# Strassen block products for half of the value, key and query projections of a hybrid decoder step

## The chip, the cores and the metric

The kernel runs on one core of a Trainium2 chip. The core has a matrix engine (TensorE, PE in the profile, with its weight loads as PEld), a vector engine (VectorE, DVE), a scalar engine (ScalarE, ACT), a general one (GpSimd, POOL), and a queue that issues transfers (SyncE, SP). On-chip data lies in SBUF, matrix results in PSUM, which has eight banks of 512 float32 columns for each of 128 partitions. The metric is the device time of one execution in microseconds (us), the median of several runs.

## The reference

One inference step of a two-layer trunk, all in float32, for a prompt of 512 tokens and 8 sample sequences of 8 tokens, 576 tokens in all (`NT`). Layer 0 is a gated short convolution, layer 1 a matrix-memory block (mLSTM). The layer that the change touches:

```python
xm, z = jnp.split(h @ w_in, 2, axis=-1)          # 1024 -> 2048 each
xc, new_buf = causal_dwconv(xm, conv_buf, conv_w)
xc = jax.nn.silu(xc + conv_b)
q = xc @ w_q                                     # 2048 -> 2048
k = xc @ w_k                                     # 2048 -> 2048
v = xm @ w_v                                     # 2048 -> 2048
gates = jnp.concatenate([q, k, v], axis=-1) @ w_if + b_if
```

After it come the chunked recurrence over four heads with a 512 x 512 state per head and sequence, a norm per head, the gate `silu(z)` and the output projection. All outputs, the new states too, are returned.

## The kernel before

Tokens lie along the free dimension (576 columns), features along the 128 partitions, so a feature vector of 2048 is 16 tiles. A weight chunk is 8 blocks of 128 x 128 (1024 inputs by 128 outputs) and arrives in one transfer of 512 KB. The values have chunks 96 to 127, two for each of 16 output tiles; keys and queries alternate in chunks 128 to 191 (tile f: key 128 + 4f and 129 + 4f, query 130 + 4f and 131 + 4f).

Every float32 product is made of three faster ones: each operand is split into a rounded high part and the low rest (`split` for activations, `split_weights` for half a chunk: a cast on ScalarE, L167, and a subtraction on VectorE, L168), and `step` issues high x high, high x low and low x high, each for 256 and 320 columns, which lie in two banks of one accumulator (L182). So a chunk is 8 k steps of 6 matmuls. The raw weights have two buffers, the split halves three each.

The stages, in program order: layer 0 (chunks 0 to 79), the input projection of layer 1 ("xm", chunks 80 to 95, with the convolution on VectorE and a store of each convolved tile to the scratch `xcs`), the values, then keys and queries head by head in the order 3, 0, 1, 2, then the z tiles, the recurrence, the state update and the output projection. The `xm` tiles stay on chip as high and low parts (32 slots of a pool of `N_SLOT` equal ones), the convolved tiles too.

Small jobs ride along: `work` is a queue from which `run` takes one job at given k steps (`pops`, two a chunk in these stages). They are the transposes of a finished tile (`by_token`), the gate products, a head's scores, and eight state products per head (`query_state`), each of which loads two halves of a state tile of 512 KB each into the pool `C` of six buffers (L135). When the key of the last tile (head 2, tile 3) is done, the first eight tiles of the residual stream come back and are normalised (`second_norm`), four ahead of the last query tile's first chunk and four ahead of its second.

The order on each engine is written by a planner when the program is built: it keeps a clock of its own, and at each time gives an engine the earliest instruction of the program that its model calls ready; a tile gets its buffer in that order too. Each engine then runs its list in order and waits at semaphores. `issue_after` pins an instruction behind another one. All loads and stores go through the one queue of SP.

Of the kernel before, what the change touches and what calls it, by code (L numbers as in the profile page):

```python
# [48 lines left out]
N_SLOT = 69  # L49
# [5 lines left out]
CBUF = 6  # L55
# [10 lines left out]
def trunk(tc, io):  # L66
    nc = tc.nc
    ctx = ExitStack()
    with ctx:
# [4 lines left out]
        cpool = ctx.enter_context(tc.tile_pool(name="cpool", bufs=CBUF))  # L74
        psum = ctx.enter_context(tc.tile_pool(name="psum", bufs=2, space=PSUM))
# [12 lines left out]
        def mm(name="mm"):  # L88
            uid[0] += 1
            return psum.tile([P, 1024], F32, name=f"{name}{uid[0]}", tag="mm", bufs=2)  # L90
# [26 lines left out]
        last_hi = []  # L117
# [38 lines left out]
        def weight_tile():  # L156
            uid[0] += 1
            return wpool.tile([P, 8, P], F32, name=f"wr{uid[0]}", tag="raw", bufs=2)

        def split_weights(raw, i, keep=False):  # L160
# [6 lines left out]
            nc.scalar.copy(hi, raw[:, 4 * i:4 * i + 4, :])  # L167
# [31 lines left out]
        def gemm(chunk0, nchunk, xs, pops=()):  # L199
            acc = mm("acc")  # L200
            for c_ in range(nchunk):
                products(acc, weights(chunk0 + c_), xs[8 * c_:8 * c_ + 8], c_ == 0, c_ == nchunk - 1, pops)
            return acc

# [43 lines left out]
        def conv(cv, u, ext, taps):  # L248
# [3 lines left out]
            nc.vector.tensor_scalar(cv, u, taps[h], None, ALU.mult)  # L252
# [21 lines left out]

        warm_up(WARM)
# [104 lines left out]
        xm, xc = [], []  # L380
# [10 lines left out]
        for f in range(NW):  # L391
# [11 lines left out]
            xm.append(split(u))  # L403
            cv = T(name="xc")
            conv(cv, u, ext_f, [col(f"cb{j}", f) for j in range(4)])
            nc.gpsimd.tensor_copy(cpb[:, f, :], u[:, NP - 3:NP])
            nc.scalar.activation(cv, cv, AF.Silu, bias=col("cbias", f))
            store(out=xcs[f], in_=cv)
            xc.append(cv)
            if f % 4 == 3:  # L410
                store(out=io["exb_out"][f // 4], in_=ext)
        store(out=io["cpb_out"], in_=cpb)
# [43 lines left out]
        xcr = xc  # L456
        xc = []
        for h in range(NH):
            vt = []
            for dt in range(4):  # L460
                f = 4 * h + dt
                acc = gemm(96 + 2 * f, 2, xm, (3, 6))
                v = T(name="v")
                nc.scalar.copy(v, flat(acc))
                vt.append(v)
                dup = S([P, 256], name="dup")
                spread(v, dup)
                s = slice(128 * dt, 128 * dt + 128)
                work.append(lambda v=v, dup=dup, h=h, s=s: by_token(v, dup, 1.0, vps[h][:, :, s], vss[h][:, :, s]))
                if f >= 8:  # L470
                    xc.append(split(xcr[f - 8]))
            work.append(lambda h=h, vt=vt: gates(h, vt))
        xc.extend(split(t) for t in xcr[8:])

        Sc, qcs = {}, {}
        nst = const.tile([P, NH, 2, 4, 4], F32, name="nst")
# [18 lines left out]
        def unit(h, u, dt):  # L495
            uid[0] += 1
            halves = []
            for i in range(2):
                t = cpool.tile([P, 2, 512], F32, name=f"c{uid[0]}_{i}", tag="C")
# [35 lines left out]
        def sample_scores(st, u):  # L535
# [5 lines left out]
            if u == 1:  # L541
# [4 lines left out]
                Sc[st["h"]] = ss  # L546
# [8 lines left out]
        heads = [dict(h=h, kt=[], qt=[], kd=[], qp=[]) for h in range(NH)]  # L555
        for h in (3, 0, 1, 2):
            st = heads[h]
            for dt in range(4):
                f = 4 * h + dt
                acc = gemm(128 + 4 * f, 2, xc, (3, 6))  # L560
                k = T(name="k")
                nc.scalar.copy(k, flat(acc))  # L562
# [8 lines left out]
                if (h, dt) == (2, 3):  # L571
                    xs = []
                    for m in range(KD):
                        x = T(name="x")
                        load(out=x, in_=x1s[m])
                        xs.append(x)
                    second_norm(range(4))
                    run(len(work))
                    acc = mm("acc")
                    products(acc, weights(128 + 4 * f + 2), xc[0:8], True, False)  # L580
# [750 lines left out]
```

## Time and profile before

| | |
|---|---|
| median of 3 runs | 1751.58 us (1749.59 to 1751.87) |
| the profiled execution, its span | 1754.37 us, 1752.6 us |
| TensorE matmuls busy, count | 1728.1 us (99%), 12771 |
| VectorE, ScalarE busy | 824.1 us (47%), 574.7 us (33%) |
| mean granted TensorE clock | 0.989 |
| moved by the transfers | 268.95 MB, mean 153 GB/s |

The span runs from the first to the last instruction; the execution's own time has a little around it. Busy shares are averages over stages with different limits. A row of a group gives line, engine, operation, the names written and read, shapes and count, then busy time and the mean of one in ns, then the idle time ahead of these instructions and what ended it. A row in order of time starts with its start and length in us. A matmul's length contains the pipeline's depth, so the distance of starts, not the length, tells its cost in a stream.

### The profile page before, as it was taken

To read this page: it belongs to the slowest core of one execution; us is meant where nothing else is said; L and a number is where in the kernel's file an instruction comes from. 1 tells how busy PE (TensorE), PEld (TensorE's weight loads), DVE (VectorE), ACT (ScalarE), POOL (GpSimd) and SP (SyncE) were. 2 spreads that over 40 slices of the span, in tenths; PEclk is the share of its full clock that TensorE was granted. 3 is DMA by queue.
4 is the path that set the end of the run, shared out by engine and by line. 5 is a ranking of instruction groups with operands and counts; after the bars stand their busy time and mean duration, and the time that the engine had idled before them with its cause. 6 is when DMAs were issued, how large, how long until landed. Compare 5 with 4: busy or idle time off the path is not lost.

```text
span 1752.6 us, 30800 instructions
## 1 busy us (share of the span) xinstructions
PE 1728.1 (99%) x12771; PEld 1654.7 (94%) x12771; DVE 824.1 (47%) x1445; ACT 574.7 (33%) x1001; POOL 125.7 (7%) x273
## 2 busy tenths in 40 slices
PE   9999999999999999999999999999999998998998
PEld 9999999999999999999999899899899887998998
DVE  5645444454346962222423222222227666678765
ACT  5222222222233332232322222222225545545421
POOL 0000000000001100000000000000001112212200
PEclk9999999999999999999999999999999899999999
DMA  5222222223343443433333543633637377997983
GB/s 165 81 86 84 89 89 85 91 79 105 125 132 104 150 139 103 120 101 108 106 88 99 192 148 94 219 125 119 211 111 247 119 227 242 370 337 265 372 304 108
DMA packets 104317, 268.95 MB, mean 153 GB/s; under 512 B 10704, under 2 KB 33104, under 8 KB 104176
## 3 DMA queue, kind: packets, MB, share of 16 engines
q1 hardware_dynamic: 104176, 266.98, 46.8%
q8 instruction: 100, 1.64, 0.4%
q14 instruction: 41, 0.34, 0.1%
HBM read 205.63 MB, written 61.30 MB: 152 GB/s over the span
## 4 chain that ended last, share of the span: by engine, by line
PE 90%; DMA 5%; DVE 3%; ACT 1%; issue 1%; SPq 0%; POOL 0%; DVEq 0%
PE acc L182 79%; DMA cs_out<-c 2%; PE qa L510 2%; DVE c L868 1%; PE r L867 1%; DMA cp_out<-cp 1%; DMA c<-cs 1%; PE g L423 1%; PE ta L442 1%; DMA wr<-wts 1%; PE cp L918 1%; PE s L529 1%; PE cp L919 1%; PE s L530 0%; DVE wl L168 0%
## 5 line engine op out<-in xcount | busy, mean ns | idle before, releaser
L182 PE MATMUL acc<-hi,wh 128*128 128x256 f32 (+1 forms) x3504 | 762.0, 299 | 6.3 <-ACT z L622 4.4
L182 PE MATMUL acc<-hi,wl 128*128 128x256 f32 (+1 forms) x3504 | 761.6, 298 | 0.0
L182 PE MATMUL acc<-lo,wh 128*128 128x256 f32 (+1 forms) x3504 | 760.2, 298 | 0.0
L182 PEld LDWEIGHTS acc<-hi,wh 128*128 128x128 f32 x3504 | 590.0, 190 | 34.5 <-issue 12.0
L182 PEld LDWEIGHTS acc<-hi,wl 128*128 128x128 f32 x3504 | 593.3, 190 | 1.8 <-issue 1.6
L182 PEld LDWEIGHTS acc<-lo,wh 128*128 128x128 f32 x3504 | 593.5, 190 | 1.2 <-issue 0.9
L168 DVE TENSOR_TENSOR wl<-wr,wh 128x512 fp32r<-128x512 f32 x438 | 305.2, 697 | 593.3 <-ACT wh L167 583.7
L167 ACT CAST wh<-wr 128x512 fp32r<-128x512 f32 x438 | 271.2, 620 | 899.5 <-PE acc L182 867.0
L868 DVE SCALAR_TENSOR_TENSOR c<-c,cols,r 128x512 f32<-128x512 f32 x128 | 91.1, 740 | 24.5 <-PE r L867 20.8
L867 PE MATMUL r<-vst,km 128*128 128x512 f32 x128 | 48.8, 441 | 6.9 <-DVE c L868 3.7
L867 PEld LDWEIGHTS r<-vst,km 128*128 128x128 f32 x128 | 23.5, 199 | 17.4 <-issue 5.3
L510 PE MATMUL qa<-c,qp 128*32 128x512 f32 x256 | 39.0, 619 | 0.0
L256 DVE SCALAR_TENSOR_TENSOR xc<-xm,cols,xc 128x511 f32<-128x511 f32 (+2 forms) x48 | 35.7, 745 | 0.0
L352 POOL COPY cpa<-u 128x2 f32<-128x2 f32 x16 | 8.9, 557 | 367.9 <-DVE u L349 367.9
L1001 POOL TENSOR_TENSOR y<-y,z 128x576 f32<-128x576 f32 x16 | 25.6, 1608 | 29.0 <-DVE y L1000 26.9
L446 ACT ACTIVATE ta<-ta 128x512 f32<-128x512 f32 x32 | 19.1, 597 | 22.7 <-PE ta L442 22.4
L358 DVE TENSOR_TENSOR cv<-acc,cv 128x576 f32<-128x576 f32 x15 | 11.4, 757 | 31.0 <-PE acc L182 31.0
L447 DVE TENSOR_SCALAR tb<-tb 128x256 f32<-128x256 f32 x32 | 13.6, 423 | 25.2 <-PE tb L444 25.2
L349 DVE TENSOR_TENSOR u<-acc,cr 128x576 f32<-128x576 f32 x15 | 11.4, 757 | 29.7 <-PE acc L182 29.7
L433 POOL COPY kd<-k 128x128 f32<-128x128 f32 x32 | 8.4, 292 | 226.0 <-ACT k L562 226.0
L331 DVE TENSOR_TENSOR cr<-acc,rb 128x576 f32<-128x576 f32 x15 | 11.3, 757 | 26.9 <-PE acc L182 26.9
L256 DVE SCALAR_TENSOR_TENSOR cv<-u,cols,cv 128x511 f32<-128x511 f32 (+1 forms) x32 | 23.9, 748 | 0.0
(291 smaller groups left out, 1502.7 us busy)
## 6 DMA issues: line engine op xcount, KB each, us to landing
wr<-wts SPq DMA_DIRECT2D x222, 512.0 KB, 3.7
c<-cs SPq DMA_DIRECT2D x112, 512.0 KB, 6.0
cs_out<-c SPq DMA_DIRECT2D x64, 512.0 KB, 7.1
x<-xT SPq DMA_DIRECT2D x16, 288.0 KB, 4.4
xcs<-xc SPq DMA_DIRECT2D x16, 288.0 KB, 2.2
x<-x1s SPq DMA_DIRECT2D x16, 288.0 KB, 6.4
ld<-xcs SPq DMA_DIRECT2D x16, 288.0 KB, 8.1
cp_out<-cp SPq DMA_DIRECT2D x16, 257.0 KB, 8.2
```

What stands on the lines that cost most here:

```text
L167: nc.scalar.copy(hi, raw[:, 4 * i:4 * i + 4, :])
L168: nc.vector.tensor_tensor(lo, raw[:, 4 * i:4 * i + 4, :], hi.bitcast(F32), ALU.subtract)
L182: nc.tensor.matmul(acc[:, o:o + j - i], a[:, k % 4, :], x[:, i:j], start=(first and k == 0 and p == 0), stop=(last and k == 7 and p == 2))
L256: nc.vector.scalar_tensor_tensor(cv[:, s:NP], u[:, 0:NP - s], taps[h - s], cv[:, s:NP], ALU.mult, ALU.add)
L423: nc.tensor.matmul(g[32 * j:32 * j + 32, 0:b - a], w[:, 32 * j:32 * j + 32], tiles[j][:, a:b], start=True, stop=True)
L442: nc.tensor.transpose(pa[:, 128 * it:128 * it + 128], t[:, 128 * it:128 * it + 128], ident)
L446: nc.scalar.activation(ta, pa, AF.Copy, scale=scale)
L510: nc.tensor.matmul(st["q"][32 * g:32 * g + 32, :], st["qp"][dt // 2][:, dt % 2, 128 * u + 32 * g:128 * u + 32 * g + 32], ct[g // 2][:, g % ...
L529: nc.tensor.matmul(sb[0], a[:, 0:128], b[:, 0:512], **ends)
L867: nc.tensor.matmul(r, kst[2 * i + j][:, 128 * dt:128 * dt + 128], vst[:, 0:512], start=True, stop=True)
L868: ins = nc.vector.scalar_tensor_tensor(ct[:, j, :], ct[:, j, :], dec[:, o + j:o + j + 1], r, ALU.mult, ALU.add).ins
L1001: nc.gpsimd.tensor_tensor(o, o, z, ALU.mult)
```

## The change

For a pair of output tiles (two value tiles, or the key and the query of one tile) the first chunk of each is now done as a 2 x 2 block product by Strassen's scheme in Winograd's form. The blocks are: output tile 1 or 2; even or odd k tile of the chunk; first or second half of the tokens (`HT` = 288). Seven block products of 4 k tiles replace eight. The second chunk of each of the two stays plain, on 288 and 288 columns, and is added in PSUM.

The activations' sums and differences (`forms`) are made once for each two of the first eight tiles; the weights' (`block_weights`, and two more in place in `block_pair`) once a pair, a pair ahead. Each weight sum is split as before (`parts_of`). The partial results are put together by VectorE from four banks (`block`), which take the place of the two accumulators in these stages.

With it come: the raw weights get four buffers and `C` four in these stages, later two and six (`load_buffers`); the conv's first tap is a scaled copy on ScalarE; an xm tile's convolution is queued as a job and done six tiles later (`LAG`); the convolved tiles are not kept but read back from `xcs`, eight of them one at a time as jobs during the values, eight at the last value pair (`mixed_blocks`); the first key-query pair does its plain half first; jobs are taken at every second k step of the plain half only; the eight tiles of `second_norm` all stand in the middle of the last pair; the scores of head 3 wait in memory (`far`) until the numerators; some small buffers move into the slots, now 74.

```diff
-N_SLOT = 69
-CBUF = 6
+N_SLOT = 74
+HT = NT // 2
+CBUF = 8
+LAG = 6
...
+        def parts_of(src):
+            uid[0] += 1
+            hi = wpool.tile([P, 4, P], F32R, name=f"wh{uid[0]}", tag="hi", bufs=3)
+            lo = wpool.tile([P, 4, P], F32R, name=f"wl{uid[0]}", tag="lo", bufs=3)
+            last_act[0] = nc.scalar.copy(hi, src).ins
+            nc.vector.tensor_tensor(lo, src, hi.bitcast(F32), ALU.subtract)
+            return hi, lo
+        def forms(xa, xb):
+            a, b = T(name="fa"), T(name="fb")
+            nc.vector.tensor_tensor(a[:, 0:HT], xa[:, 0:HT], xa[:, HT:NT], ALU.subtract)
+            nc.vector.tensor_tensor(a[:, HT:NT], xb[:, HT:NT], a[:, 0:HT], ALU.add)
+            nc.vector.tensor_tensor(b[:, 0:HT], xa[:, HT:NT], xb[:, HT:NT], ALU.subtract)
+            nc.vector.tensor_tensor(b[:, HT:NT], xb[:, 0:HT], a[:, HT:NT], ALU.subtract)
+            o = R(name="hl")
+            nc.scalar.copy(o[:, 0:HT], xa[:, 0:HT])
+            nc.vector.tensor_tensor(o[:, HT:NT], xa[:, 0:HT], o[:, 0:HT].bitcast(F32), ALU.subtract)
+            (ah, al), (bh, bl), (xh, xl) = split(a), split(b), split(xb)
...
+        def block_weights(c1, c2):
+            r1, r2 = weight_tile(), weight_tile()
+            for r, c_ in ((r1, c1), (r2, c2)):
+                latest[0] = load(out=r, in_=io["wts"][c_]).ins
+            a11, a12, a21, a22 = [r[:, i:8:2, :] for r in (r1, r2) for i in range(2)]
+            s1, s2 = [T(512, name="ws").rearrange("p (k x) -> p k x", x=P) for _ in range(2)]
+            nc.vector.tensor_tensor(s1, a21, a22, ALU.add)
+            nc.vector.tensor_tensor(s2, s1, a11, ALU.add)
...
+        def block_pair(c1, c2, fs, xs, out1, out2, add, mid=None, then=None):
...
+            def product(bank_, w, form, start):
+                for j in range(4):
+                    hi, lo = fs[j][form]
+                    for i, (a, x) in enumerate(((w[0], hi), (w[0], lo), (w[1], hi))):
+                        nc.tensor.matmul(bank_, a[:, j, :], x, start=(start and j == 0 and i == 0), stop=(j == 3 and i == 2),
+                                         skip_group_check=True)
+            b1 = block("p6")
+            product(b1, parts_of(s2), "t2", True)
+            b0 = block("p1")
+            product(b0, parts_of(a11), "b11", True)
+            nc.scalar.copy(p, b0)
+            b2 = block("p5")
+            product(b2, parts_of(s1), "t1", True)
...
+                tt(o12, p, b1, ALU.subtract)
+            product(b0, parts_of(a12), "b21", False)
...
+                tt(o22, p, b2, ALU.add)
+            tt(a21, a21, a11, ALU.add)
+            tt(s2, s2, a12, ALU.add)
+            product(b1, parts_of(a21), "t3", False)
+            b3 = block("p4")
+            product(b3, parts_of(a22), "t4", True)
+            tt(u, b1, p, ALU.subtract)
...
+                tt(o22, b1, o22, ALU.subtract)
+            product(b2, parts_of(s2), "b22", False)
+            if mid:
+                mid()
+            if then:
+                block_weights(*then)
...
+                plain(b3, b1, c2 + 1, xs, False)
+                tt(o21, b3, u, ALU.add)
+                tt(o22, b1, o22, ALU.add)
+                plain(b0, b2, c1 + 1, xs, None)
+                nc.scalar.copy(o11, b0)
+            tt(o12, o12, b2, ALU.add)
+        def plain(ba, bb, chunk, xs, start):
+            w = weights(chunk)
+            for k in range(8):
+                (hi, lo), (xh, xl) = w[k // 4], xs[k]
+                for i, (a, x) in enumerate(((hi, xh), (hi, xl), (lo, xh))):
+                    for b, t in ((ba, 0), (bb, HT)):
...
+                        nc.tensor.matmul(b, a[:, k % 4, :], x[:, t:t + HT], start=bool(new) and k == 0 and i == 0,
+                                         stop=(k == 7 and i == 2), skip_group_check=True)
+                if k % 2:
+                    run()
...
-            nc.vector.tensor_scalar(cv, u, taps[h], None, ALU.mult)
+            nc.scalar.activation(cv, u, AF.Copy, scale=taps[h])
...
-                acc = gemm(96 + 2 * f, 2, xm, (3, 6))
+                gemm_pair(96 + 2 * f, 98 + 2 * f, fm, xm, *pair, mid=mixed_blocks if f == NW - 2 else None,
+                          then=(100 + 2 * f, 102 + 2 * f) if f < NW - 2 else (176, 178))
...
-                acc = gemm(128 + 4 * f, 2, xc, (3, 6))
+                gemm_pair(128 + 4 * f, 130 + 4 * f, fc, xc, k, q, plain_first=(h, dt) == (3, 0),
+                          mid=next_stage if (h, dt) == (2, 3) else None,
```

More of the change, by code (lines that the diff above doesn't have):

```diff
@@ new lines, in gemm_pair @@
+        def gemm_pair(c1, c2, fs, xs, out1, out2, plain_first=False, mid=None, then=None):
+            if (c1, c2) not in ahead_of:
+                block_weights(c1, c2)
+            if plain_first:
+                for c_, o in ((c1, out1), (c2, out2)):
+                    ba, bb = block(), block()
+                    plain(ba, bb, c_ + 1, xs, True)
+                    nc.scalar.copy(o[:, 0:HT], ba)
+                    nc.scalar.copy(o[:, HT:NT], bb)
+            block_pair(c1, c2, fs, xs, out1, out2, plain_first, mid, then)
@@ L273, in warm_up @@
             return ins
+        accumulators("acc0", bufs=2)
+        load_buffers("loads0", 4)
         warm_up(WARM)
@@ L555, in trunk @@
         heads = [dict(h=h, kt=[], qt=[], kd=[], qp=[]) for h in range(NH)]
+        order = [4 * h + dt for h in (3, 0, 1, 2) for dt in range(4)]
         for h in (3, 0, 1, 2):
@@ L559, in trunk, with next_stage @@
                 f = 4 * h + dt
-                acc = gemm(128 + 4 * f, 2, xc, (3, 6))
-                k = T(name="k")
-                nc.scalar.copy(k, flat(acc))
+                k, q = T(name="k"), T(name="q")
+                def next_stage():
+                    for m in range(KD):
+                        x = T(name="x")
+                        load(out=x, in_=x1s[m])
+                        xs.append(x)
+                    run(len(work))
+                    second_norm(range(KD))
+                if (h, dt) == (2, 3):
+                    xs = []
+                gemm_pair(128 + 4 * f, 130 + 4 * f, fc, xc, k, q, plain_first=(h, dt) == (3, 0),
+                          mid=next_stage if (h, dt) == (2, 3) else None,
+                          then=next(((128 + 4 * g, 130 + 4 * g) for i, g in enumerate(order) if i and order[i - 1] == f), None))
                 st["kt"].append(k)
@@ L570, in trunk @@
                     kss[h][:, :, 128 * dt:128 * dt + 128]))
[L571 to L580, printed above, removed]
-                    second_norm(range(4, KD))
-                    products(acc, weights(128 + 4 * f + 3), xc[8:16], False, True)
-                else:
-                    acc = gemm(128 + 4 * f + 2, 2, xc, (3, 6))
-                q = T(name="q")
-                last_q = nc.scalar.copy(q, flat(acc))
+                last_q = last_act[0]
                 st["qt"].append(q)
```

148 lines of the change are left out of this document (110 added, 38 removed).

## The prediction

> **What bounds the kernel now.** I read the page first, then busy time by stretch, then TensorE in order of time, then the groups, the chain and the transfers. The page:
>
> ```profile
> span 1752.6 us, 30800 instructions
> PE 1728.1 (99%) x12771; PEld 1654.7 (94%) x12771; DVE 824.1 (47%) x1445; ACT 574.7 (33%) x1001; POOL 125.7 (7%) x273
> PE 90%; DMA 5%; DVE 3%; ACT 1%; issue 1%; SPq 0%; POOL 0%; DVEq 0%
> ```
>
> TensorE is 90% of the chain that ended last. A busy TensorE need not be at its peak, so the stages matter (columns: stretch; length; PE, PEld, DVE, ACT, POOL busy with instruction counts; granted clock; DMA share; GB/s):
>
> ```profile
> 550.00:575.00 25.00, 25.00 (x190) 25.00 (x189) 25.00 (x56) 9.97 (x16) 3.05 (x4) 1.00 0.43 135
> 625.00:650.00 25.00, 25.00 (x191) 25.00 (x190) 15.46 (x32) 8.88 (x15) 1.10 (x3) 1.00 0.54 156
> 650.00:675.00 25.00, 25.00 (x192) 25.00 (x191) 6.22 (x10) 7.24 (x12) 1.04 (x4) 1.00 0.40 110
> 1125.00:1150.00 25.00, 25.00 (x184) 19.90 (x183) 4.15 (x6) 4.26 (x7) 0.53 (x2) 1.00 0.74 258
> 1325.00:1350.00 25.00, 25.00 (x183) 21.37 (x182) 22.18 (x38) 18.28 (x35) 6.45 (x13) 1.00 0.71 250
> 1375.00:1400.00 25.00, 25.00 (x129) 17.86 (x128) 11.10 (x16) 9.82 (x20) 0.00 (x0) 0.81 0.38 128
> 1400.00:1425.00 25.00, 25.00 (x152) 20.45 (x152) 17.30 (x39) 8.79 (x17) 4.39 (x9) 0.85 0.61 197
> 1650.00:1675.00 25.00, 21.70 (x131) 19.17 (x131) 20.77 (x28) 8.88 (x15) 6.19 (x4) 0.93 1.03 390
> ```
>
> ```profile
> 645.14 12.14 PE acc L182 x91
> ...
> 1338.29 3.41 PE acc L182 x24
> ```
>
> The value, key and query products lie between about 630 and 1338: in the chain, the piece behind the first value tile's transposes starts at 645, in the second tile, and the first z tile's at 1338. There TensorE runs without a gap at clock 1.00 while VectorE is a quarter busy (6.22 of 25 us). VectorE is full only in the xm stage (550:575) and at the end of the queries (1325:1350), and TensorE keeps its count there too. After 1375 the picture is another one: fewer matmuls, lower clock, DMA full. The change touches the middle, where a matmul less should be time less. What a matmul is worth, from TensorE in order of time (start, length, what):
>
> ```profile
> 560.20 0.43 PE L182 MATMUL acc<-lo,wh 128*128 128x256 f32 x2
> 560.46 0.43 PE L182 MATMUL acc<-hi,wl 128*128 128x256 f32 x2
> 560.73 0.43 PE L182 MATMUL acc<-hi,wh 128*128 128x256 f32 x2
> ...
> 1720.33 0.31 PE L182 MATMUL acc<-hi,kh 128*128 128x320 f32 x1
> ...
> 1730.74 0.31 PE L182 MATMUL acc<-hi,kl 128*128 128x320 f32 x1
> 1730.89 0.28 PE L182 MATMUL acc<-hi,kh 128*128 128x256 f32 x1
> ...
> 1731.49 0.28 PE L182 MATMUL acc<-hi,kl 128*128 128x256 f32 x1
> ```
>
> A 256 and a 320 column matmul together start every 0.267 us (560.20 to 560.73 is two such pairs). Alone, the 320 column ones start 0.1466 apart (72 of them, first and last shown) and the 256 column ones 0.12 (six rows, five steps in 0.60). That is columns at 2.4 per ns plus 13.3 ns, so 288 columns, half way, take 0.1333 us, and splitting 576 tokens into 288+288 rather than 256+320 costs nothing.
>
> **The change part by part.** *Removed matmuls.* Two output tiles over one chunk each were 2 x 8 x 3 x 2 = 96 matmuls; seven block products of 4 x 3 are 84. The other chunk of each stays at 96 in all. So a pair goes from 25.6 to 24.0 us, and there are 8 value pairs and 16 key-with-query pairs: 24 x 12 x 0.1333 = **38.4 us** off. Every block product matmul has its own weight load, but so has every matmul now (x12771 for both), and the stretch from 1720 changes weights in the same 2:1 rhythm.
>
> The page "TensorE: Matmul & The Clock Gate" of the Trainium skill (section "Back-to-back issue gap") gives columns/2.4 + 2.5 ns, 122.5 ns here, and the sum by it would be 35.3 us. The trace has 0.267 us for 576 columns, so the trace decides; the rule leaves out a part of the weight load that this kernel pays.
>
> *Added vector and scalar work per pair.* The prices:
>
> ```profile
> L168 DVE TENSOR_TENSOR wl<-wr,wh 128x512 fp32r<-128x512 f32 x438 | 305.2, 697 | 593.3 <-ACT wh L167 583.7 <-PE acc L182 4.7 <-ACT e L750 2.7
> L167 ACT CAST wh<-wr 128x512 fp32r<-128x512 f32 x438 | 271.2, 620 | 899.5 <-PE acc L182 867.0 <-issue 22.6 <-DMA wr<-wts 5.9
> L252 DVE TENSOR_SCALAR xc<-xm,cols 128x576 f32<-128x576 f32 x16 | 8.2, 515 | 0.0
> L124 DVE TENSOR_TENSOR lo<-xc,hi 128x576 fp32r<-128x576 f32 x16 | 11.6, 754 | 3.5 <-ACT hi L123 2.5 <-POOL dup L433 1.0
> L551 DVE SCALAR_TENSOR_TENSOR x<-x,cols,rb 128x576 f32<-128x576 f32 x8 | 6.4, 816 | 2.0 <-DMA x<-x1s 1.8
> ...
> 1335.94 0.42 DVE L428 TENSOR_TENSOR gacc<-g,gacc 128x256 f32<-128x256 f32 x1
> 1336.94 0.49 DVE L428 TENSOR_TENSOR gacc<-g,gacc 128x320 f32<-128x320 f32 x1
> ```
>
> Seven weight sums are split in place of four (+3 casts at 0.620, +3 subtractions at 0.697), four additions of 512 columns make the sums (0.697), and seven operations of 288 columns out of PSUM gather the result. No row has 288; between the two L428 rows it is 0.46. VectorE gains 3 x 0.697 + 4 x 0.697 + 7 x 0.46 = 8.1 us on a pair of 24 us, and goes from a quarter to some 60%. ScalarE gains under 2 us. By throughput all this is hidden. By order it is tighter: a product lasts 12 x 0.1333 = 1.6 us where half a chunk lasted 3.2, and the split weights have three buffers. The cast for a product can start when the product three before it has ended, 3.2 us ahead of need; cast plus subtraction take 1.32, and up to two results of 0.46 or one sum of 0.697 may stand in front on VectorE. That is 2.3 of 3.2, with the low part needed only by the third matmul. Bounds: nothing, and 0.23 us a product (the loss rival below). The slack is nearer the first: 2 us for all 168 products. The bank of P1 must be copied before the next product on it; one 1.6 us product lies between, and a copy of 576 takes 0.64 us even in full.
>
> *From the input projection to the values.* The forms of eight tiles cost four pairs x (5 x 0.46 + 3 x 0.754) = 18.2 us instead of 8 x 0.754 = 6.0; the first tap on ScalarE takes 16 x 0.515 = 8.2 off VectorE, and six convolutions wait until the values. That load is about even, under 16 x 6.4 = 102 us of TensorE. What waits is the first product's bank: the old accumulator pool must be emptied by the last multiplication, behind one running operation. Bounds: 0, and three operations of 0.754, 2.2 us; I take 1.
>
> *From values to keys and queries.* The convolved tiles come back from memory (16 loads of 288 KB), eight of them and their forms only at the last value pair, because the slots come free there. This is 18.2 us of VectorE, written ahead of the weight splits of 12.8 us of plain products, with 12.8 more plain after that (the first key pair does its plain half first). If the splits wait behind all of it, three buffered halves (9.6 us) stand against 18.2 us. Bounds: 0 and 8.6; the two covers together exceed the work, so I take 3.
>
> *State loads in the queries' stage.* Four state buffers in place of six, and eight jobs spaced two k steps apart in the plain half rather than spread. Now (chain in order of time, then the state tile from 985 to 1030):
>
> ```profile
> 993.47 1.00 PE qa L510 x8
> 994.46 2.59 PE acc L182 x18
> 997.05 1.00 PE qa L510 x8
> 998.05 4.19 PE acc L182 x30
> ...
> L135 SPq DMA_DIRECT2D c<-cs x10: 327/356/426, 994.5 to 1012.5; - x10
> DMA to landing us min/median/max: 4.0/4.9/6.2
> ```
>
> A state unit comes every 3.6 or 5.2 us and none waits. After the change its place comes every 1.6 + 1.0 = 2.6 us; with two units of buffers the load of unit n+2 starts at the end of unit n and has 4.2 us, against 4.9 to 6.2 for landing. In written order that is a wait of 0.7 to 2.0 us per two units, three times a head, three heads: 6 to 18 us. But the planner lets ready work pass:
>
> ```profile
> 1346.65 0.53 PE acc L182 x4
> 1349.06 0.57 PE acc L182 x4
> 1350.87 0.72 PE acc L182 x5
> ```
>
> Here the program has eighteen matmuls of a z tile between two score jobs, and the chain shows runs of four or five between them. So bounds 0 and 18, and I take 2: a wait is left only where the planner's load time is too short.
>
> *From the queries to the z tiles.* All eight tiles of the second norm now stand ahead of 12.8 us of plain products, where four stood ahead of the last query tile and four in its middle.
>
> ```profile
> wr<-wts SPq DMA_DIRECT2D x222, 512.0 KB, 3.7
> x<-x1s SPq DMA_DIRECT2D x16, 288.0 KB, 6.4
> ```
>
> Landing 6.4 + 8 x (0.816 + 0.754) = 19.0 us against 12.8 plus 5.6 until the last k step asks: 0.6 short, and plain splits, results and z weights (4 x 0.697 + 3 x 0.46 + 2 x 0.697 = 5.6) compete. Bounds 0 and 6, taken 2, since scores of head 2 can fill in as above. A plain chunk's raw buffer comes free some 3.3 us into a pair (1.6 until the first product's split buffer is free, 1.32 for the split that reads it last, and a result in front) and is needed at 9.9 (11.2 less 1.32), against 3.7 us of landing: nothing. If that cover were gone, each pair would wait for the 3.7.
>
> *The tail.* Three score tiles of head 3 go to memory and back: 3 x 262 KB at the 390 GB/s of the fullest row is 2.0 us of transfers. Bounds 0 (a gap in the DMA) and 2.0; I take 1.
>
> **The sum.** -38.4 + 2 + 1 + 3 + 2 + 2 + 1 = -27.4. The profiled execution took 1754.4 (span 1752.6 and 1.8 around it), so 1727.0; the median of the runs is 2.8 lower, so **1724 us**. With every cost at zero it is 1713; another 2 us may fall off where the z stage packs otherwise. With every boundary and state bound at its far end (2.2 + 8.6 + 18 + 6 + 2.0 = 36.8) and the products at nothing it is 1750.
>
> **The rivals.** *Given back at the boundaries.* About half of that 36.8, 18 to 27 us, comes true: 1731 to 1740, middle 1736, still faster. For it: VectorE already at 22.18 of 25 around 1325, and the tight state buffers. Against it: TensorE's counts stay whole in the very stretches where VectorE is full.
>
> *The weight feed becomes the bound (slower).* Place: the wait of each product's first matmul on its cast and subtraction. If cast, subtraction and results in front take more than the 3.2 us of two products, TensorE waits at each. The break-even is 38.4/168 = 0.23 us a product. At 0.4 us it is 67 us, so 1754.4 - 38.4 + 67 - 2.8 = 1780. For it: the sums, splits and results hang on each other through three engines, in an order fixed at build time. Against it: 2.3 of 3.2 us by the rows, and VectorE's subtraction now waits 583.7 us on casts, that is, on buffers, not on its own speed.
>
> *The clock falls.* Short waits between products in four rotating banks bring the granted clock down, as in 1400:1425, where 0.85 goes with x152. At 0.85 the 24 x 11.2 = 269 us of products take 47 us more: 1754.4 - 38.4 + 47 - 2.8 = 1760. The same page, section "A second HAM failure mode: psum-queue depth-cycling", describes such a loss. In this trace the accumulators rotate too, at clock 1.00 from 25 to 1375, and the drops come only where matmuls are missing, so the trace gives this little room.
>
> *The tail takes it back.* From 1375 on transfers set much of the pace (share 1.03, 390 GB/s at 1650). If the state stream, not TensorE, decided the end, an earlier start would be lost. But the stream's loads start with the z stage and would start earlier as well, and TensorE still has 131 or more matmuls in each stretch: 1751.
>
> **How the numbers follow.** Forecast 0.66; given back at the boundaries 0.17; feed as the bound 0.10; clock 0.03; tail 0.04. About 3.5 us (0.2%) is what a measurement of this kernel can tell from no change. Faster is 0.66 + 0.17 = 0.83, same 0.04, slower 0.13. The range 1711 to 1750 runs from the zero-cost end, with its 2 us, to the far end of all boundary bounds, and leaves out the slower cases and the tail: about 0.17.
>
> **What would show it.** Block products starting a matmul every 0.133 us and pairs about 24 us apart (plus transposes), at clock 1.00, show the gain; some 288 matmuls fewer must be counted. Casts waiting on TensorE more than TensorE on casts and subtractions show the feed holds. Waits of TensorE at the last value pair, at the state products, or between the last query and the first z tile size the other terms. I am wrong if TensorE waits over 0.2 us at most products, if the state products wait for loads, or if the stage from the first z tile on becomes more than 10 us longer.

## The result, and the profile after

The changed kernel takes 1769.24 us in the median of four runs (1765.65 to 1771.56), the kernel before, beside it, 1751.72 us (1749.59 to 1754.33). The ratio is 1.0098, with a 95% interval of 1.0075 to 1.012: 1% slower, where 1.6% faster was forecast. Stages and waits below are read from one profiled execution of each kernel, and a few us of one stage can be chance: executions of the kernel before differ by up to 8 us (1747.10 us at a mean granted clock of 0.993, 1755.11 at 0.988), and one of ten of the kernel "buffers out" below, of 3315.24 us, is left out of its ratio.

The profiled execution of the changed kernel took 1769.84 us. The lines of its page that answer to those shown of before:

```profile
span 1768.0 us, 30952 instructions
PE 1721.9 (97%) x12483; PEld 1622.2 (92%) x12483; DVE 1001.7 (57%) x1800; ACT 637.0 (36%) x1124; POOL 147.4 (8%) x273
PE 87%; DMA 5%; DVE 3%; ACT 2%; issue 1%; SPq 0%; POOL 0%; DVEq 0%; ACTq 0%; POOLq 0%
```

The 288 matmuls are gone (12771 to 12483), yet TensorE's busy time fell by 6.2 us only, and the span grew by 15.4. VectorE has 178 us more work and stands at 57%. So the loss is partly time in which TensorE counts as busy, partly new waits. Busy time by stretch of the changed kernel (columns as in the prediction) shows where it is:

```profile
550.00:575.00 25.00, 24.00 (x180) 24.03 (x181) 19.77 (x41) 9.76 (x18) 2.34 (x5) 1.00 0.28 88
625.00:650.00 25.00, 19.38 (x129) 18.47 (x128) 24.57 (x53) 12.56 (x21) 0.58 (x1) 0.89 0.31 103
700.00:725.00 25.00, 25.00 (x191) 24.32 (x190) 14.00 (x26) 8.65 (x16) 1.35 (x4) 1.00 0.37 116
1000.00:1025.00 25.00, 25.00 (x151) 15.98 (x151) 8.36 (x16) 4.41 (x8) 2.79 (x7) 1.00 0.77 250
1600.00:1625.00 25.00, 18.37 (x121) 17.75 (x120) 20.06 (x26) 16.14 (x30) 7.72 (x6) 0.86 0.44 139
```

and the kernel before in one of them:

```profile
1000.00:1025.00 25.00, 25.00 (x184) 19.00 (x183) 3.78 (x7) 4.12 (x7) 0.73 (x3) 1.00 0.67 236
```

In the middle of the values (700) there are 191 matmuls in 25 us at clock 1.00; before has 192 there. At the start of the values (625) there are 129, where before had 191. In the queries with state products (1000) TensorE is busy throughout, but with 151 instructions; before had 184 in the same stretch. In the tail (1600) it works for 18.37 of 25 us, at a mean clock of 0.86.

The stages, each from its first matmul to the next stage's first, from TensorE in order of time (us; "k3" is the key and query stage of head 3, and so on; "tail" runs from the first z matmul to the start of the last matmul of the kernel). The columns behind the second are experiments told below:

| stage | before | after | joined units | lag 2 | buffers out | all three |
|---|---|---|---|---|---|---|
| xm | 104.8 | 107.4 | 107.4 | 108.6 | 107.4 | 108.6 |
| values | 218.4 | 212.8 | 212.8 | 206.5 | 212.5 | 206.8 |
| k3 | 106.9 | 100.4 | 100.4 | 100.4 | 100.4 | 100.1 |
| k0 | 126.8 | 128.2 | 122.5 | 128.2 | 127.7 | 122.3 |
| k1 | 126.8 | 128.4 | 122.3 | 128.2 | 127.8 | 121.9 |
| k2 | 128.9 | 131.6 | 125.7 | 132.8 | 133.2 | 126.5 |
| tail | 410.9 | 431.0 | 423.6 | 425.0 | 412.4 | 404.8 |

By the price of the matmuls, the values should fall by 8 x 1.6 = 12.8 us and each of the four heads by 6.4. Against that, the changed kernel gave back 2.6 in xm, 7.2 at the values, nothing in k3, 7.8, 8.0 and 9.1 in the other heads, and 20.1 in the tail: -38.4 + 2.6 + 7.2 - 0.1 + 24.9 + 20.1 = 16.3. The first xm matmul came 0.8 earlier, so that is the 15.4 of the span. Three places are to be explained: the heads 0, 1 and 2, the start of the values, and the tail.

### The profile page after: what moved, and what is told of

It reads as the page before. It is cut to its first block, busy times and chain, and to the rows that moved or that the text cites. A ratio compares the mean times of both kernels' runs of the same rounds, so it can differ in the third digit from the quotient of the medians.

```text
span 1768.0 us, 30952 instructions
## 1 busy us (share of the span) xinstructions
PE 1721.9 (97%) x12483; PEld 1622.2 (92%) x12483; DVE 1001.7 (57%) x1800; ACT 637.0 (36%) x1124; POOL 147.4 (8%) x273
## 4 chain that ended last, share of the span: by engine, by line
PE 87%; DMA 5%; DVE 3%; ACT 2%; issue 1%; SPq 0%; POOL 0%; DVEq 0%; ACTq 0%; POOLq 0%
PE acc L209 43%; PE p L339 17%; PE p L283 15%; PE qa L687 3%; DMA wr<-wts 1%; DMA cs_out<-c 1%; PE g L589 1%; DMA cp_out<-cp 1%; DMA c<-cs 1%; PE ta L608 1%; PE r L1050 1%; DVE c L1051 1%; PE blk L339 1%; PE s L706 1%; PE cp L1101 1%
## 5 line engine op out<-in xcount | busy, mean ns | idle before, releaser
L209 PE MATMUL acc<-hi,wh 128*128 128x256 f32 (+1 forms) x1968 | 427.8, 299 | 15.2 <-ACT z L803 10.9
L209 PE MATMUL acc<-hi,wl 128*128 128x256 f32 (+1 forms) x1968 | 426.9, 298 | 0.0
L209 PE MATMUL acc<-lo,wh 128*128 128x256 f32 (+1 forms) x1968 | 425.7, 298 | 0.0
L209 PEld LDWEIGHTS acc<-hi,wh 128*128 128x128 f32 x1968 | 333.9, 191 | 20.3 <-ACT z L803 11.4
L209 PEld LDWEIGHTS acc<-hi,wl 128*128 128x128 f32 x1968 | 333.2, 191 | 1.6 <-issue 0.7
L209 PEld LDWEIGHTS acc<-lo,wh 128*128 128x128 f32 x1968 | 333.2, 191 | 1.0 <-issue 0.8
L283 PE MATMUL p<-hi,wh 128*128 128x288 f32 x576 | 171.9, 299 | 0.9 <-DVE xm L556 0.9
L283 PE MATMUL p<-hi,wl 128*128 128x288 f32 x576 | 172.3, 300 | 0.0
L283 PE MATMUL p<-lo,wh 128*128 128x288 f32 x576 | 169.9, 295 | 0.0
L339 PE MATMUL p<-hi,wh 128*128 128x288 f32 x736 | 163.9, 300 | 1.2 <-ACT wh L194 1.2
L339 PE MATMUL p<-hi,wl 128*128 128x288 f32 x736 | 158.9, 298 | 3.5 <-DVE wl L195 3.5
L339 PE MATMUL p<-lo,wh 128*128 128x288 f32 x736 | 160.7, 297 | 0.0
L339 PEld LDWEIGHTS p<-lo,wh 128*128 128x128 f32 x736 | 119.9, 190 | 2.5 <-issue 2.5
L283 PEld LDWEIGHTS p<-hi,wl 128*128 128x128 f32 x576 | 108.1, 188 | 7.2 <-DVE q L313 2.5
L283 PEld LDWEIGHTS p<-lo,wh 128*128 128x128 f32 x576 | 108.2, 188 | 3.4 <-issue 3.4
L283 PEld LDWEIGHTS p<-hi,wh 128*128 128x128 f32 x576 | 108.2, 188 | 1.7 <-ACT wh L237 1.1
```

Of the source, the lines that this page charges most:

```text
L209: nc.tensor.matmul(acc[:, o:o + j - i], a[:, k % 4, :], x[:, i:j], start=(first and k == 0 and p == 0), stop=(last and k == 7 and p == 2))
L283: nc.tensor.matmul(bank_, a[:, j, :], x, start=(start and j == 0 and i == 0), stop=(j == 3 and i == 2), skip_group_check=True)
L339: nc.tensor.matmul(b, a[:, k % 4, :], x[:, t:t + HT], start=bool(new) and k == 0 and i == 0, stop=(k == 7 and i == 2), skip_group_check=True)
```

## The experiments

Every kernel was run beside the kernel before on the same chip.

### The state units, joined

In order of time on TensorE (start, length, what), before has whole state units of eight matmuls, and the changed kernel mostly halves of four (six of the eight units of each head). First before, then after:

```profile
993.40 1.06 PE L510 MATMUL qa<-c,qp 128*32 128x512 f32 x8
996.98 1.07 PE L510 MATMUL qa<-c,qp 128*32 128x512 f32 x8
```

```profile
998.79 1.06 PE L687 MATMUL qa<-c,qp 128*32 128x512 f32 x8
...
1007.00 1.05 PE L687 MATMUL qa<-c,qp 128*32 128x512 f32 x4
1007.99 0.53 PE L339 MATMUL p<-lo,wh 128*128 128x288 f32 x2
...
1009.35 1.05 PE L687 MATMUL qa<-c,qp 128*32 128x512 f32 x4
```

A half takes as long as a whole unit. A unit is four column groups of 32 with two matmuls each; in one row they run side by side, and a half has only two of the groups. The Trainium skill, "TensorE: Matmul & The Clock Gate", section "Packing small matmuls — row/col tiling", says that matmuls on different tiles of the array run at the same time; by that rule a half costs what a whole does, and the trace agrees (1.05 against 1.06 us). The experiment is the changed kernel with the groups of the second half first and the other two pinned right behind them, so that the whole unit goes out at once when both halves have landed:

```diff
-            for g in range(4):
-                nc.tensor.matmul(st["q"][32 * g:32 * g + 32, :], ...)
+            hold = nullcontext
+            for g in (2, 3, 0, 1) if st["h"] != 2 else range(4):
+                with hold():
+                    ins = nc.tensor.matmul(st["q"][32 * g:32 * g + 32, :], ...).ins
+                if st["h"] != 2 and g == 3:
+                    hold = lambda: tc.issue_after(ins)
```

> The changed kernel with one edit: of each state unit of heads 3, 0 and 1 the two matmuls on the second half are written first and the two on the first half are pinned behind them, so that the four column groups of a unit are issued together. Theory (split units): in the changed trace a half unit (4 rows) holds TensorE 1.05 us, as long as a whole one (8 rows), and the state products of a head take 13.8 us in place of 8.0; joined they take 8.0 again, each of the heads 0, 1, 2 gets 5.8 us shorter (128.2 to about 122.5), and the time falls by about 17 to 1752. Rival (late loads): four buffers are too few, the joined units wait for their later half instead, TensorE's idle time takes the place of the split, and the time stays within 5 us of 1769.

Measured: 1744.47 us (1743.46 to 1745.34), ratio 0.9955 [0.994, 0.997]. The busy time of the state products alone from 985 to 1335 us, of before, of after and of this kernel:

```profile
985.00:1335.00 350.00, 25.57 (x192) 1.00 0.47 154
```

```profile
985.00:1335.00 350.00, 44.27 (x192) 1.00 0.51 164
```

```profile
985.00:1335.00 350.00, 28.69 (x192) 1.00 0.53 175
```

The same 192 matmuls took 18.7 us more in the changed kernel, and all but 3.1 of it comes back when the units are joined; one unit of each head still goes out as six and two. The three heads fell by 17.7 us in the stage table, which is most of the 24.9 that they had given back. Of the other 7.2, the distances of starts put 2.6 on the gate products (3.1 us in each of heads 0 and 1, where before has 2.2; 5.1 for 4.3 in head 2). A further 7.4 us fell off the tail, in which this edit changes nothing. There was hardly a wait for data behind the cost of the halves: TensorE's waits of the whole changed kernel (waiting instruction, what it waited for; us, times, longest) have one wait of a state product for its load:

```profile
PE acc L209 <- ACT z L803: 10.9, 2, 6.6
...
PE p L339 <- DVE wl L195: 3.5, 1, 3.5
...
PE acc L209 <- DVE xm L556: 1.3, 1, 1.3
PE p L339 <- ACT wh L194: 1.2, 2, 1.0
PE qa L687 <- DMA c<-cs: 1.1, 1, 1.1
...
PE p L283 <- DVE xm L556: 0.9, 1, 0.9
```

### Four state buffers in the kernel before

Which edit parted the halves? The kernel before with four state buffers, nothing else:

```diff
-CBUF = 6
+CBUF = 4
```

> The kernel before with four state buffers in place of six, nothing else. If four buffers alone part the halves of a state unit (the second half's load must wait for a half of the unit two before), three of the eight units of a head come apart, each costing about (13.8 - 8.0)/8 = 0.73 us: the state products of a head take 8.0 + 3 x 0.73 = 10.2 us, the three heads 6.5 us in all, and the median is 1752 + 6 = 1758 us (1754 to 1760). If the close spacing of the jobs in the plain half parts the halves and not the number of buffers, the heads keep 8.0 us and the median is 1752 (1750 to 1754).

Measured: 1773.33 us (1769.57 to 1774.44) against 1749.38, ratio 1.0125 [1.0101, 1.0149]. The state products alone:

```profile
985.00:1335.00 350.00, 34.92 (x192) 1.00 0.46 152
```

Three units of each head came apart, as its instruction list has it, and cost 9.35 us of TensorE's busy time together, 1.04 each: a second half's full price, not the 0.73 that was expected (that had spread a head's excess over all eight units, where six are parted). Heads 0, 1 and 2 took 130.2, 130.2 and 132.3 us, 3.4 more each. In the changed kernel the excess is 18.7 us, or six units of eight per head at this price. So the buffers alone part three, and it is the closer spacing of the jobs, argued and not run by itself, that parts the other three. So the first case holds, with a larger price. A further 7.9 us was not foreseen: the tail grew from 410.9 to 418.8, with four buffers there as well.

### The start of the values, with a shorter lag

The changed kernel's first value pair, in order of time on all engines:

```profile
628.97 0.37 PE L283 MATMUL p<-hi,wh 128*128 128x288 f32 x1 [0.94 <-DVE xm L556]
...
636.66 4.10 ACT L404 ACTIVATE xc<-xm,cols 128x576 f32<-128x576 f32 x6
...
640.67 1.64 ACT L194 CAST wh<-wr 128x512 fp32r<-128x512 f32 x3
...
645.88 0.68 DVE L195 TENSOR_TENSOR wl<-wr,wh 128x512 fp32r<-128x512 f32 x1
...
646.61 0.85 PE L339 MATMUL p<-hi,wl 128*128 128x288 f32 x2 [3.46 <-DVE wl L195]
```

and the stretches around it:

```profile
641.00:646.00 5.00, 1.60 (x8) 1.13 (x8) 5.00 (x13) 1.31 (x3) 0.00 (x0) 0.86 0.00 0
646.00:651.00 5.00, 4.39 (x18) 4.39 (x19) 5.00 (x11) 0.00 (x0) 0.00 (x0) 0.50 0.38 108
651.00:656.00 5.00, 5.00 (x38) 5.00 (x37) 5.00 (x13) 4.08 (x7) 0.00 (x0) 0.95 0.38 146
```

The six convolutions that wait for the values do their first taps on ScalarE in one block of 4.10 us, ahead of the casts of the plain chunk, and their other taps fill VectorE, ahead of the subtractions. TensorE waits 3.46 us, and then works at half clock: 18 matmuls in the 5 us after 646, where 38 fit in the next 5. Against 38, the two stretches miss 30 and 20 matmuls, 4.0 and 2.7 us at 0.133: nearly all of the 7.2. The same page of the Trainium skill, section "What's actually happening", says that an idle window of about 3.4 us halves TensorE's clock. The trace agrees with the halving (0.50), but not with a window that is wholly idle: the mean of 0.86 over the first stretch puts the start of the half clock at about 644.6, some 1.5 us into the wait, and the stretch from 641 to there holds eight matmuls. So the shorter waits ahead had their part in it. The edit lets a tile's convolution come two tiles later in place of six:

```diff
-LAG = 6
+LAG = 2
```

> The changed kernel with LAG 2 in place of 6: a tile's convolution is queued two tiles behind, so two and not six are left when the values begin. Theory (queued convolutions): the 4.1 us of six first taps on ScalarE and the taps on VectorE that stood ahead of the first plain chunk's splits at 636 to 646 go, with them the waits of 1.0 and 3.5 us there and the half clock of 6.8 us behind them; the values' stage gets some 7 us shorter and the time falls to about 1762. Rival (VectorE is simply too full): the same wait moves into the xm stage, that stage gets as much longer as the values get shorter, and the time stays at 1769.

Measured: 1760.85 us, ratio 1.0048 [1.0033, 1.0063]. The stretch at the start of the values:

```profile
625.00:650.00 25.00, 22.69 (x165) 21.77 (x164) 23.49 (x49) 14.27 (x23) 0.59 (x1) 1.00 0.36 120
650.00:675.00 25.00, 25.00 (x192) 25.00 (x191) 13.55 (x26) 8.67 (x16) 1.33 (x4) 1.00 0.46 144
```

The half clock and the 3.46 us wait are gone, the values' stage fell by 6.3 to 206.5 us, 0.9 short of the full gain, and xm rose by 1.2. Another 6.0 us fell off the tail, for which this edit gives no reason of its own.

### The tail edits, without the block products

First, the kernel before with what the change does to the tail: the scores of head 3 kept in memory, and the small buffers (the state's rounded copy `sth`, the key stack `kst`, `dup`) in the slots, 74 of them.

> The kernel before with those edits of the change that touch the part after the queries, and no block products: the scores of head 3 go to memory and back, the small buffers of the stacks and of the duplicated sample columns move into the slots, 74 of them. Theory (the edits cost): the part from the first z tile to the end, 411 us before and 431 after, takes about 431 here, and the time is about 1772. Rival (another plan): the edits cost under 5 us, the part takes 411 to 416, the time is 1752 to 1757, and the 20 us come from how the part is entered and ordered.

Measured: 1766.98 us, ratio 1.0087 [1.007, 1.0104]. Every stage ahead of the tail kept its time; the tail grew from 410.9 to 421.3. Then the other way round: the changed kernel with block products for the values alone, keys and queries as before, head 3's scores on chip, but the small buffers in the slots.

> The changed kernel with block products for the values alone; keys and queries by whole chunks as before, no spill of the scores, six state buffers again from the keys on. Theory (three separate losses): 8 x 1.6 = 12.8 us are saved on TensorE, about 10 are given back at the start of the values and in the xm stage, the state products are whole (8.0 us a head), so the keys begin some 3 us earlier than before and the time is about 1748 if the last part keeps its 411 us. Rival (the block products themselves cost): the values' stage is not shorter than before by more than 2 us even without its first pair.

Measured: 1770.68 us, ratio 1.0102 [1.0087, 1.0117]. The keys and queries take what they took before (107.7, 126.8, 126.8, 128.9), the values 214.3, and the tail 428.7. So the tail's loss needs neither the block products of the keys nor the scores in memory. The two tail edits apart, each on the kernel before; the buffers:

```diff
-N_SLOT = 69
+N_SLOT = 74
...
-                dup = S([P, 256], name="dup")
+                dup = T(256, name="dup")
...
-            hi = S([P, 512], F32R, "sth")[:, 0:src.shape[1]]
+            hi = R(512, "sth")[:, 0:src.shape[1]]
...
-            o = S([P, 512], F32R, "kst", 3)
+            o = R(512, "kst")
```

> The kernel before with one edit of the change: the buffers of the stacks (rounded copy and key stack) and of the duplicated sample columns come from the common slots, 74 in place of 69, the same memory. Theory (the slots cost): with tail edits together the last part took 421.3 in place of 410.9 us, and the rise came between 165 and 225 us into it, in the kernel without the spill too; so the slots alone give most of it, a last part of 417 to 422 and a time of 1759 to 1765. Rival (the spill costs): under 3 us from the slots, a time of 1751 to 1755.

and the scores:

```diff
+        far = [dram.tile([P, 512], F32, name=f"far{i}") for i in range(3)]
...
+                if st["h"] == 3:
+                    for t, d in zip(ss, far):
+                        store(out=d, in_=t)
+                else:
+                    Sc[st["h"]] = ss
...
+            if h not in Sc:
+                Sc[h] = fetched.pop(("S", h))
...
+            if h == 0:
+                fetch(("S", 3), *far)
```

> The kernel before with the other edit alone: the scores of head 3 go to memory and come back during head 0, slots and small buffers as before. Theory (the slots cost): 3 x 262 KB at 390 GB/s are 2 us, the last part takes 411 to 414 us, the time 1751 to 1756. Rival (the spill costs): a last part near 421 and a time near 1764.

Measured: the buffers 1769.12 us, ratio 1.0098 [1.0081, 1.0116], tail 424.9; the scores 1760.02, ratio 1.0038 [1.0024, 1.0051], tail 416.3. The buffers alone cost 14.0 us of tail, the scores 5.4, and both together 10.4: the two don't add.

### All three repairs, and the buffers out

Two kernels were run with the joined units, a lag of two and the gate products' four groups pinned together; the second of them also gives `dup`, `sth` and `kst` their own buffers again, the diff above the other way round (69 slots).

> The changed kernel with the joined state units and LAG 2 together, and the four column groups of each gate product pinned in one order (the group that is ready last first). Theory: the edits act in different stages and add up: the values take 206.5 us as with LAG 2, heads 0 to 2 some 122 each less about 0.9 of split gate products, the z tiles begin at about 1302 to 1306, and with a last part of 423 us the time is about 1734. Rival: the last part takes back what is gained (it ends on transfers), so that the time stays at the 1744 of the joined units alone.

> The same kernel with the stack buffers and the duplicated columns out of the slots again, so 69 slots. Theory (the slots cost): the last part falls by about 10 us to some 413, while five slots fewer cost the value and query stages little, since their tiles come free in turn; time about 1725. Rival: with 69 slots the forms and the read-back tiles wait at the values' end and in the queries, those stages get longer by more than 10 us, and the time is above that of the joined kernel with 74.

Measured: 1745.19 us (1744.54 to 1748.68), ratio 0.9964 [0.9951, 0.9977], and with the buffers out 1723.43 us (1722.34 to 1727.87), ratio 0.9839 [0.9819, 0.986]. The first is no better than the joined units alone (1744.47): what the lag gave in the values the tail took (429.2 us). The second has a tail of 404.8, shorter than that of before, and the kernel beats both others. Its page:

```profile
span 1720.5 us, 30956 instructions
PE 1690.1 (98%) x12483; PEld 1609.4 (94%) x12483; DVE 999.4 (58%) x1800; ACT 638.6 (37%) x1124; POOL 150.7 (9%) x273
```

Pinning the gate products did nothing that can be seen: they took some 3 us in each of the heads 0 and 1 with it and without it.

Last, the buffers out of the changed kernel and nothing else:

> The changed kernel with one part undone: the state's rounded copy, the key stack and the small copies have their own buffers again (69 slots in place of 74), the state units stay in halves, the six-tile lag stays. If the moved buffers are what lengthens the tail, the stage from the first z tile on falls from 431 us by about the 24 us that the joined kernel lost in the same way, the middle keeps its times (state products 13.8 us a head), and the median is 1769 - 22 = 1747 us (1743 to 1752). If that gain came from the two edits together, from another packing of the tail that hangs on where the z stage starts, it falls by less than 10 us: over 1759 us.

Measured: 1749.89 us against 1749.38, ratio 0.9997 [0.9982, 1.0012]. The middle kept its times within 1.6 us a stage, and the tail fell by 18.6 to 412.4. So the first case holds: without this one edit the change would have made no difference, with it it is 1% slower. Over the tail alone, before, after, after with the buffers out, and the kernel with all three repairs (columns as in the prediction; from the first z matmul to the end of the last matmul):

```profile
1334.90:1746.10 411.20, 395.44 (x2712) 359.46 (x2709) 280.67 (x515) 188.52 (x369) 59.67 (x74) 0.96 0.75 262
```

```profile
1330.20:1761.50 431.30, 400.35 (x2709) 362.64 (x2705) 283.90 (x513) 185.05 (x362) 59.81 (x68) 0.95 0.75 251
```

```profile
1331.80:1744.40 412.60, 391.67 (x2709) 356.09 (x2705) 284.53 (x513) 186.20 (x363) 61.16 (x68) 0.97 0.76 263
```

```profile
1308.60:1713.70 405.10, 388.56 (x2709) 354.69 (x2705) 281.16 (x513) 185.87 (x363) 61.07 (x68) 0.98 0.77 268
```

TensorE is idle for 15.8, 31.0, 20.9 and 16.5 us of these. So of what the moved buffers cost here, some 10 us are waits of TensorE, and some 9 are the same 2709 matmuls at a lower mean clock (0.95 for 0.97). The tail with all three repairs is shorter than that of before with no less idle time, by its clock (0.98 for 0.96).

### One buffer at a time

The key stack alone, then the rounded copy alone, in the slots of the kernel before (71 and 70 slots):

> The kernel before with the key stack alone in the slots (71 slots for 69; three buffers of its own given up). All three small buffers together cost 17.4 us. If the key stack, which the numerators of every head wait for, carries most of it: 1752 + 10 to 17, 1762 to 1769 us. If the state's rounded copy carries it: 1752 within 4 us here, and the 10 to 17 us in the run of the copy alone. If it is a matter of the packing as a whole and no single buffer's: both within 8 us of 1752, either way.

> The kernel before with the state's rounded copy alone in the slots (70 slots for 69; two buffers of its own given up). If the copy, which takes and gives back a slot for every half of a state tile, carries most of the 17.4 us: 1762 to 1769 us. If the key stack carries it: 1752 within 4 us. If it is the packing as a whole: within 8 us of 1752, either way.

Measured: the key stack 1776.36 us, ratio 1.0143 [1.0117, 1.0169], tail 434.8; the copy 1771.59, ratio 1.0115 [1.0091, 1.014], tail 424.0. None of the three cases expected this: the copy alone costs about what all together cost, the stack alone more. What they share shows on VectorE. The second key stack, in order of time, in before, after, after with the buffers out, and before with only the stack in the slots:

```profile
1401.05 0.75 DVE L770 SCALAR_TENSOR_TENSOR kst<-sth,cst,ld 128x512 fp32r<-128x512 f32 x1
```

```profile
1416.94 0.75 DVE L953 SCALAR_TENSOR_TENSOR kst<-sth,cst,ld 128x512 fp32r<-128x512 f32 x1
```

```profile
1395.78 0.75 DVE L953 SCALAR_TENSOR_TENSOR kst<-sth,cst,ld 128x512 fp32r<-128x512 f32 x1
```

```profile
1420.60 0.74 DVE L770 SCALAR_TENSOR_TENSOR kst<-sth,cst,ld 128x512 fp32r<-128x512 f32 x1
```

The first z matmul of these four starts at 1334.9, 1330.2, 1331.8 and 1335.2, so the stack is made 66, 87, 64 and 85 us into the tail. Taken over all fourteen kernels: in the five with own buffers (before, scores in memory, four state buffers, and the two with the buffers out) the second stack is made 63 to 69 us into the tail, and the tail lasts 404.8 to 418.8 us; in the nine with the stack, or the copy that it is made from, in the slots it is made 84 to 90 us into it, and the tail lasts 421.3 to 434.8. The written order shows the same from the first key stack on: in the list of VectorE's instructions of the kernel with the stack in the slots, against that of before (the part around the first stack, buffer numbers left out), it has moved behind six others; the second stack stands 25 places later.

```diff
-L770 SCALAR_TENSOR_TENSOR kst<-sth,cst,ld 128x512
 L168 TENSOR_TENSOR wl<-wr,wh 128x512
 L888 TENSOR_TENSOR vl<-ld,vh 128x512
 L888 TENSOR_TENSOR vl<-ld,vh 128x512
+L168 TENSOR_TENSOR wl<-wr,wh 128x512
 L888 TENSOR_TENSOR vl<-ld,vh 128x512
-L168 TENSOR_TENSOR wl<-wr,wh 128x512
+L888 TENSOR_TENSOR vl<-ld,vh 128x512
+L770 SCALAR_TENSOR_TENSOR kst<-sth,cst,ld 128x512
```

Behind the stack come the masked keys, the state's products, the new state's stores, and the loads of further state halves into the same buffers. The queue's waits in the tail (for the store of a state half before the next load into its buffer; us, times, longest), of before, after, and after with the buffers out:

```profile
SPq L135 <- DMA cs_out<-c: 54.3, 26, 6.5
```

```profile
SPq L163 <- DMA cs_out<-c: 74.9, 34, 6.6
```

```profile
SPq L163 <- DMA cs_out<-c: 58.5, 27, 6.5
```

They are longer in the changed kernel, but they don't follow the late stack: with four state buffers in the kernel before they are 79.3 us and its stack is early, and in the kernel with joined units, a lag of two and the buffers in the slots they are 53.2 us, with a stack 90 us into a tail of 429.2. TensorE itself waits for a key stack for 0.4 us only in the changed kernel (PE pn L989 <- DVE kst L953 in its list of waits). That the planner gives the stack its slot late, because in a full pool it stands behind tiles that come earlier in the program, is how the planner works and not measured by itself. That the late stack is what costs the time is not shown: in these fourteen kernels it comes with the buffers in the slots and never without, so their split can't tell it from another effect of the slots. What is shown is that the buffers in the slots cost the time. How much hangs on the rest of the plan (10 to 24 us), and why the scores in memory cost 5.4 us in the kernel before, but nothing that shows in the changed kernel with the buffers out (tail 412.4 and 404.8, scores in memory in both), stays open.

## Why the prediction was wrong

*Removed matmuls, -38.4: right.* 288 fewer are counted, and block products start a matmul every 0.133 us:

```profile
713.11 0.30 PE L283 MATMUL p<-hi,wh 128*128 128x288 f32 x1
713.24 0.29 PE L283 MATMUL p<-lo,wh 128*128 128x288 f32 x1
713.38 0.29 PE L283 MATMUL p<-hi,wl 128*128 128x288 f32 x1
...
713.91 0.29 PE L283 MATMUL p<-hi,wh 128*128 128x288 f32 x1
```

The stage of head 3, which has no state products, fell by 6.5 us, four pairs at 1.6. The price of 122.5 ns, by the formula of the Trainium skill's page "TensorE: Matmul & The Clock Gate" (section "Back-to-back issue gap", which gives it for an isolated matmul), would have made it 5.9.

*The products' feed, 2: right in kind, too high.* In the list of waits above, the block products' line L283 has one wait of 0.9 us, and that at the start of the values; head 3's stage gave back nothing. The rival of the feed, and that of a clock falling in the products, are false: 191 matmuls in 25 us at 1.00.

*From the input projection to the values, 1 of 0 to 2.2: wrong.* It measured 9.8 (2.6 in xm, 7.2 in the values). The step priced a bank that is emptied late, and that wait was 0.9. It named the six queued convolutions, but weighed that load as a sum over 102 us of TensorE and not by the order on the two engines: they came in one block ahead of the plain chunk's casts and subtractions, and the waits were long enough for the clock to be halved. Of the 2.6 us in xm, 1.3 is a wait for the tile's own result (in the list above); the rest was not located.

*From values to keys, 3: too high.* Head 3's stage shows nothing of it.

*State loads, 2 of 0 to 18: wrong in kind.* The prediction looked for a wait for loads. There was one, of 1.1 us. What came instead was that the planner, with four buffers and (argued, as said above) close jobs, "lets ready work pass" between the halves of a unit, and each parted unit cost another 1.04 us: 18.7 us of TensorE's busy time. The price of 1.0 us a unit was a price for eight matmuls issued together, and the prediction carried it over to a change which took that away. So one of its own signs, state products waiting for loads, showed nothing, while TensorE counted as busy throughout.

*From the queries to z, 2: near.* Head 2 gave back 9.1 us where heads 0 and 1 gave back 7.8 and 8.0: about 1.

*The tail, 1 of 0 to 2.0: wrong.* It measured 20.1. The prediction priced three score tiles' transfers, and gave the small buffers that move into the slots no price and no bound. With them back in their own buffers the tail of the changed kernel fell by 18.6. The sign that was named, a tail more than 10 us longer, came true.

The rival that half of the boundary costs come true was the nearest in kind, but the boundaries' bounds did not hold these costs: the state products' cost came as busy time where a wait was bounded, and the moved buffers had no term. The rival that the tail takes an earlier start back is false in its mechanism: with all three repairs the first z matmul comes 26.3 us earlier than in before, and the span is 32.1 us shorter. That this kernel ends at 1723.43 us, beside a forecast of 1724, is in part luck: its stages ahead of the tail gain 26.4 us, near the 28.4 that the forecast had there after its costs, but it needed three edits that the forecast did not have, and its tail is 6.1 us shorter, by its clock, where the forecast had 1 us more.

## What to carry to other kernels

A price read from instructions that go out side by side holds only while they do: when a change touches what keeps them together (buffers for their loads, the spacing of jobs), price them alone as well, and look for it in busy time, not in waits. A buffer moved into a shared pool is not free even if the memory is: ask which work was done ahead in it, how late that work comes when it has to queue for a slot, and give the move a term of its own. And where a planner writes the order, compare stages and not totals, since edits in the tail did not add up here (14.0 and 5.4 us apart, 10.4 together).

## What the runs showed of the hardware

Four matmuls on two column groups took 1.05 us and eight on four groups 1.06. Around a wait of 3.46 us TensorE's granted clock fell to 0.50, from about 1.5 us into the wait, though eight matmuls had run in the 3.4 us before; it was 0.50 in the 5 us from 646 on, which hold the wait's end at 646.61, and 0.95 in the 5 after that, so the half clock cost about 2 us beyond the wait itself (20 matmuls fewer than 38 at 0.133 us, less the 0.6 us of the wait that lie in that stretch).
